# Attention's fill work in a hybrid encoder layer: casts placed behind their loads, the last gate by channels, early sigmoids in stage one, two y tiles kept on chip

## The chip, the cores and the metric

The kernel runs on one core of a Trainium2 chip. Its engines have queues of their own: PE (TensorE) multiplies, ACT (ScalarE) evaluates functions, casts and copies, DVE (VectorE) and POOL (GpSimd) do elementwise work, and SP (SyncE) issues every DMA here, in order. The metric is the device time of one execution in microseconds (us).

## The reference, cut to what matters

One layer with S = D = 1024 and 16 heads of 64. Heads 0 to 7 are softmax heads over a band of keys (branch A), heads 8 to 15 are stick-breaking heads (branch B). Each branch is projected back to 1024 channels and multiplied by a sigmoid gate of its own.

```python
h = x @ w_in[l]
qa, ka, va, qb, kb, vb, ga, gb = jnp.split(h, split_pts, axis=-1)
y_a = chunk_band_attention(heads_a(qa), heads_a(ka), heads_a(va), rel_bias[l]) @ w_proj_a[l]
y_b = stick_breaking_attention(heads_b(qb), heads_b(kb), heads_b(vb)) @ w_proj_b[l]
gate_a = jax.nn.sigmoid(ga + b_gate[l, :D])
gate_b = jax.nn.sigmoid(gb + b_gate[l, D:])
mix = (gate_a * y_a + gate_b * y_b) @ w_out[l]
x = layer_norm(DEEPNORM_ALPHA * x + mix, ln1_g[l], ln1_b[l])
gu = x @ w_ffn_in[l]
g, u = jnp.split(gu, 2, axis=-1)
ffn = (jax.nn.silu(g) * u) @ w_ffn_out[l]
x = layer_norm(DEEPNORM_ALPHA * x + ffn, ln2_g[l], ln2_b[l])
```

A stick-breaking weight is a sigmoid of the score times the running product of one minus the sigmoids between key and query.

## The kernel before, in words

All operands are float32. A product is emulated by three matmuls of the type fp32r: each operand is split into a high part (a cast, on ACT) and a low part (the difference, on DVE or POOL). `split` (L108 to 110) does both. So each weight and each activation tile that PE is to read costs a cast on ACT and a subtraction elsewhere, after its load.

Stage one (0 to some 348 us) projects x to q, k and v of all heads and to ten of the sixteen gate tiles (`project`, `run_pairs`; pairs of column blocks share their seven products as in Strassen's scheme). Results go to DRAM tiles: q_dr, k_dr, v_dr, and g_dr for the gates, as raw sums, by `out_g` (L363 and 364). Its last five pairs are gate pairs, A's tile and B's tile of the same channels c = 0 to 4.

Attention (some 348 to 676 us) goes through the heads in order. One unit computes 128 queries of one head: `scores` (two matmuls, L464 and 465), for a softmax head a bias with a minimum on DVE (L501), exp on ACT (L507) and a division on POOL (L512); for a stick-breaking head two sigmoids on ACT (L539 kp, L540 w), a running product on DVE (L542, L545) and a multiplication on POOL (L547). Then `value_steps` transposes blocks of the weights on PE (`turn`, L570), splits them on ACT and DVE (the pt tiles, L109 and L110), and multiplies by v (`mult`, L583 and 584) into the single PSUM bank pv. At the end of a half the pv bank is copied by ACT (L598; for the last pair L590), half of it changes partitions by DMA (L599), and POOL adds it into the y tile (L602), three steps later, through the list `later`. The finished y tile of a pair of heads, 128 channels by 1024 positions, is stored to y_dr (L604). Pairs 0 to 3 are branch A, 4 to 7 branch B; the last one (y7) stays on chip.

Attention's own PE work leaves PE free, so a generator, `fill_all`, gives PE other matmuls in between; `fill_until` takes from it as many as the constants FILL allow in each step. The fill work is, in this order: the six gate tiles 10 to 15 (`gate`, 48 matmuls each, over eight channels tiles of x), then branch A's projection, eight output tiles c = 0 to 7 of 24 matmuls (L630), each multiplied by its gate gA on DVE (L633). Its inputs come through:

- `load_w`: DMA of a weight tile, the cast (L404) and the subtraction (L405), all emitted at one place. `load_gate` and `load_proj` call it one tile ahead of use.
- `reload_y` (L651 to 657): DMA of a y tile from y_dr, cast on ACT, subtraction on POOL. y0 to y3, branch A's, are reloaded behind gate 15, into the slots that x's split tiles held; y4, y5 and y6 one after each second output tile.
- `reload_gate` (L659 to 662): DMA of a gate tile from g_dr and the sigmoid with its bias on ACT.

After attention, the yB stage (to some 705 us) projects branch B, applies its gates gB through the same `reload_gate`, and adds branch A; then come w_out, LayerNorm, the feed-forward block and the second LayerNorm.

On-chip tiles come from tagged slots (SLOTS) and PSUM banks (BANKS), taken in rotation: who takes a slot waits until its last user is done. Within an engine, instructions run in the order that the scheduler of the framework gives them from the order of the program and its own estimates. So an instruction that waits holds up everything behind it in its engine's queue.

Of the kernel before, what the change touches and what calls it, by code (L numbers as in the profile page):

```python
# [11 lines left out]
F32 = mybir.dt.float32  # L12
F32R = mybir.dt.float32r
AF = mybir.ActivationFunctionType
ALU = mybir.AluOpType
# [32 lines left out]
def hybrid_trunk_kernel(ctx: ExitStack, tc, x, xt, w_in, b_gate, rel_bias, w_proj,  # L48
# [202 lines left out]
    xh = [slot("xt", f"xh{k}", F32R) for k in range(KT)]  # L251
    xl = [slot("xt", f"xl{k}", F32R) for k in range(KT)]
# [72 lines left out]
    def project(i):  # L325
# [37 lines left out]
        def out_g(side):  # L363
            dma(g_dr[2 * pair + int(side) - 1], tl[side])
# [32 lines left out]
    def load_w(srcs, name, raw, hl, lo_eng):  # L397
        r = raw(f"wr_{name}")
        hi = hl(f"wh_{name}", F32R)
        lo = hl(f"wl_{name}", F32R)  # L400
        srcs = srcs if isinstance(srcs, list) else [(slice(0, 1024), srcs)]
        for cs, src in srcs:
            dma(r[:, cs], src)
        nc.scalar.copy(hi, r)  # L404
        lo_eng.tensor_tensor(lo, r, hi.bitcast(F32), ALU.subtract)  # L405
        return hi, lo
# [4 lines left out]
    def load_gate(i, lo_eng):  # L411
        return load_w(w_in[24 + (i % 2) * 8 + i // 2], f"g{i}", of("op"), of("op"), lo_eng)

    def gate(i, w):
        gt = slot("gt", f"gate{i}")
        for hf, cs in enumerate((LO, HI)):
            acc = bank("mm", f"gps{i}_{hf}")
            for k in range(KT):
                ks = slice(k * P, (k + 1) * P)
                for j, (lw, rx) in enumerate(((w[0], xh), (w[0], xl), (w[1], xh))):  # L420
                    mm(acc, lw[:, ks], rx[k][:, cs], start=(k == j == 0),  # L421
                       stop=(k == KT - 1 and j == 2))
                    yield 1.0
            nc.scalar.copy(gt[:, cs], acc)
# [9 lines left out]
    first_w = load_gate(first_gate, nc.vector)  # L434
# [116 lines left out]
    def value_steps(hd, g, wt):  # L551
# [9 lines left out]
        for i, kb in enumerate(kbs):  # L561
# [14 lines left out]
            def mult(i=i, kb=kb, lo_q=lo_q, n=n, pts=pts):  # L576
# [8 lines left out]
                if last:  # L585
# [6 lines left out]
                    else:  # L592
# [8 lines left out]
                        def add():  # L601
                            nc.gpsimd.tensor_tensor(yt[r, gs], yt[r, gs], yv[r, gs], ALU.add)  # L602
                            if h == 1 and g == 1:
                                dma(y_dr[hd["i"]], yt)  # L604
# [6 lines left out]
    def fill_all():  # L611
        w = first_w
        for i in range(first_gate, 16):
            nxt = load_gate(i + 1, nc.gpsimd) if i < 15 else load_proj(0, 0, "op", nc.gpsimd)
            yield from gate(i, w)
            w = nxt
        for i in range(4):
            reload_y(i, nc.gpsimd)
        for cc in range(4):
            nxt = load_proj(0, cc + 1, "op", nc.gpsimd) if cc < 3 else None  # L620
            for j in range(2):
                c = 2 * cc + j
                t = slot("gt", f"gA{c}")
                reload_gate(t, c, 0)
                for hf, cs in enumerate((LO, HI)):
                    acc = bank("mm", f"yAps{c}_{hf}")
# [498 lines left out]
```

## Time and profile before

| what | us |
|---|---|
| median of three runs | 1466.01 |
| lowest, highest | 1466.0, 1467.67 |
| profiled execution | 1465.81 |
| its span | 1464.0 |
| PE busy in the span | 1432.2 |
| ACT busy | 679.4 |
| POOL busy | 278.1 |

The mean granted clock of PE in the profiled execution is 0.995 of full. A line of a timeline reads: start, duration, engine, line of the code, operation, output tile, input tile, shapes, count, and in brackets the idle time of the engine ahead of it with what ended that. A line of the waits reads: who waited for whom, microseconds in total, times, the longest.

### The profile page before, as it was taken

The page shows a single profiled execution, that of the slowest core. Times are in us where ns is not written, and L with a number is a line of the kernel's source. Part 1 is how long each engine was busy: PE and PEld are TensorE (multiplying, and loading weights), DVE is VectorE, ACT ScalarE, POOL GpSimd, SP SyncE. Part 2 cuts the span into 40 slices and gives each one's busy share as a digit, 9 for nine tenths or more (in the row PEclk, how much of TensorE's full clock was granted, in tenths as well). Part 3 has the DMA queues.
Part 4 walks back from the last instruction along what each step waited for, and adds up shares of the span by engine and source line. Part 5 has one row for each costly group of instructions (what it writes and reads, how often), then busy time and mean ns, then how long its engine had stood idle before and what let it go on. Part 6 is the DMA issues. An engine that isn't in the chain of part 4 may idle for free.

```text
span 1464.0 us, 19115 instructions
## 1 busy us (share of the span) xinstructions
PE 1432.2 (98%) x6740; PEld 1184.4 (81%) x6740; DVE 1025.3 (70%) x1637; ACT 679.4 (46%) x1179; POOL 278.1 (19%) x326
## 2 busy tenths in 40 slices
PE   8999999999999998999999999999999999999997
PEld 6788888887888787878888888888888888888886
DVE  8856655434776876887848966777776665978767
ACT  6444444335878878775413534444444433221201
POOL 0000000003555879760004100000000000100016
PEclk9999999999999999999999999999999999999999
DMA  6565545338666476856611123444444457887602
GB/s 216 158 188 173 157 145 177 124 99 249 188 196 206 131 217 184 238 179 247 232 43 72 50 95 130 158 154 148 152 151 145 152 195 247 301 308 235 213 15 101
DMA packets 83455, 247.72 MB, mean 169 GB/s; under 512 B 10512, under 2 KB 10512, under 8 KB 83360
## 3 DMA queue, kind: packets, MB, share of 16 engines
q1 hardware_dynamic: 83360, 246.51, 51.5%
q8 instruction: 53, 0.87, 0.3%
q14 instruction: 42, 0.34, 0.1%
HBM read 162.03 MB, written 80.77 MB: 166 GB/s over the span
## 4 chain that ended last, share of the span: by engine, by line
PE 86%; DVE 5%; DMA 3%; ACT 3%; issue 2%; POOL 1%; SPq 0%; POOLq 0%; DVEq 0%; ACTq 0%
PE sxf L171 16%; PE sxp L171 12%; PE szf L171 8%; PE dx L1058 6%; PE szp L171 6%; PE syf L171 4%; PE gps L421 3%; PE dz L1058 3%; PE syp L171 3%; PE yAps L630 2%; PE ops L117 2%; PE ops L119 2%; PE ops L116 2%; PE fpswh_h L119 1%; PE fpswh_h L116 1%
## 5 line engine op out<-in xcount | busy, mean ns | idle before, releaser
L1014 POOL TENSOR_TENSOR wdyt<-wdyt 128x512 f32<-128x512 f32 x8 | 10.8, 1352 | 513.6 <-DMA wdgt<-in_w_ffn_out_dram 429.1
L547 POOL TENSOR_TENSOR w_b<-w_b,kp_b 128x511 f32<-128x511 f32 (+3 forms) x96 | 96.2, 1010 | 39.0 <-DVE kp_b L542 27.0
L542 DVE TENSOR_TENSOR_SCAN kp_b<-kp_b,ident_ps 128x512 f32<-128x512 f32 (+2 forms) x64 | 56.4, 883 | 24.8 <-ACT kp_b L539 24.3
L482 POOL MEMSET bias<- 64x64 f32 x8 | 1.2, 144 | 329.7 <-ACT bias L481 329.7
L778 POOL TENSOR_TENSOR mv<-mv,neghalf 128x1 f32<-128x1 f32 x16 | 23.8, 1489 | 210.3 <-DVE mv L777 210.3
L184 DVE TENSOR_TENSOR c<-sxp,c 128x512 f32<-128x512 f32 x16 | 11.1, 691 | 74.2 <-issue 41.1
L539 ACT ACTIVATE kp_b<-sc_b 128x512 f32<-128x512 f32 (+3 forms) x96 | 50.0, 521 | 24.9 <-PE sc_b L465 23.2
L110 DVE TENSOR_TENSOR pt_b<-tp_b,pt_b 128x512 fp32r<-128x512 f32 (+1 forms) x96 | 50.4, 543 | 13.8 <-ACT pt_b L109 13.5
L989 DVE TENSOR_TENSOR x<-dx,x 128x512 f32<-128x512 f32 x64 | 43.5, 686 | 17.0 <-PE dx L1058 16.9
L171 PE MATMUL szf<-x1S63h,wcf 128*128 128x512 f32 x168 | 55.1, 389 | 0.0
L109 ACT CAST pt_b<-tp_b 128x512 fp32r<-128x512 f32 (+1 forms) x96 | 48.2, 515 | 7.7 <-PE tp_b L570 6.1
L110 DVE TENSOR_TENSOR sl<-h,sl 128x512 fp32r<-128x512 f32 x56 | 38.4, 685 | 18.8 <-ACT sl L109 18.8
L512 POOL TENSOR_SCALAR w_a<-w_a,st_a 128x640 f32<-128x640 f32 (+2 forms) x64 | 42.6, 670 | 45.1 <-DVE st_a L511 33.5
L109 ACT CAST sl<-h 128x512 fp32r<-128x512 f32 x56 | 34.7, 619 | 34.5 <-PE syf L171 17.1
L110 DVE TENSOR_TENSOR pt_a<-tp_a,pt_a 128x512 fp32r<-128x512 f32 (+1 forms) x96 | 45.8, 486 | 6.8 <-ACT pt_a L109 5.5
L540 ACT ACTIVATE w_b<-sc_b 128x511 f32<-128x511 f32 (+3 forms) x96 | 50.2, 523 | 0.0
L570 PE MATMUL tp_b<-ident,w_b 128*128 128x128 f32 x288 | 48.7, 279 | 1.5 <-DVE pt_b L110 1.1
L116 PE MATMUL ops<-wh_o,mh 128*128 128x512 f32 x128 | 50.2, 392 | 0.0
L119 PE MATMUL ops<-wh_o,ml 128*128 128x512 f32 x128 | 50.0, 391 | 0.0
L117 PE MATMUL ops<-wl_o,mh 128*128 128x512 f32 x128 | 49.9, 390 | 0.0
L109 ACT CAST pt_a<-tp_a 128x512 fp32r<-128x512 f32 (+1 forms) x96 | 39.7, 426 | 19.2 <-PE tp_a L570 17.8
L507 ACT ACTIVATE w_a<-w_a,st_a 128x640 f32<-128x640 f32 (+2 forms) x64 | 44.7, 698 | 6.4 <-DVE st_a L501 5.9
(1883 smaller groups left out, 4811.4 us busy)
## 6 DMA issues: line engine op xcount, KB each, us to landing
s_dr<-sl SPq DMA_DIRECT2D x112, 256.0 KB, 2.1
sd<-s_dr SPq DMA_DIRECT2D x56, 512.0 KB, 4.5
wLf<-in_w_ffn_in_dram SPq DMA_DIRECT2D x22, 512.0 KB, 4.3
wRf<-in_w_ffn_in_dram SPq DMA_DIRECT2D x22, 512.0 KB, 3.6
wLp<-in_w_in_dram SPq DMA_DIRECT2D x17, 512.0 KB, 5.4
wRp<-in_w_in_dram SPq DMA_DIRECT2D x17, 512.0 KB, 4.2
v_dr<-v SPq DMA_DIRECT2D x16, 512.0 KB, 4.6
qs<-q_dr SPq DMA_DIRECT2D x16, 512.0 KB, 5.3
```

What stands on the lines that cost most here:

```text
L109: nc.scalar.copy(dst_h, src)
L110: nc.vector.tensor_tensor(dst_l, src, dst_h.bitcast(F32), ALU.subtract)
L116: mm(acc, lh, rh, start=(i == 0), stop=False)
L117: mm(acc, lh, rl, start=False, stop=False)
L119: mm(acc, ll, rh, start=False, stop=(i == n))
L171: mm(acc, lw[:, ks], rx, start=(first and kt == i == 0), stop=(kt == 3 and i == 2), skip_group_check=not first)
L539: nc.scalar.activation(kp[:, c0:e], sc[:, 0:n], AF.Sigmoid, scale=-1.0)
L540: nc.scalar.activation(be[:, m0:e], sc[:, m0 - c0:n], AF.Sigmoid)
L542: nc.vector.tensor_tensor_scan(kp[:, 0:e], kp[:, 0:e], ident_ps()[:, 0:e], 0.0, ALU.mult, ALU.add)
L547: nc.gpsimd.tensor_tensor(be[:, m0:e], be[:, m0:e], kp[:, m0 - 1:e - 1], ALU.mult)
L570: tr(tp[:, (qb - lo_q) * P:(qb - lo_q + 1) * P], wt[qb - q0][:, (kb - qb) * P:(kb - qb + 1) * P], ident)
L1058: mm(acc, a, b, start=(first and i == n == 0), stop=(i == n - 1 == 1), skip_group_check=not first)
```

## The change

- `load_w` is cut in two: `begin_w` issues the DMA, and the function that it returns emits the cast and the subtraction. For gate weights that function is called half-way through the tile before; for branch A's projection weights at the second output tile of a pair.
- Gate 15 is computed by channels in both of its halves at once, each half in an mm bank. As soon as a channel tile k of x has been used in both, `freed(k)` starts the load of y_k (k below 4), and the split follows two channels later. The split tiles of x are allocated in pairs (xh0, xl0, xh1, ...), so that y_k takes the slots of x's channel k.
- `out_g` applies bias and sigmoid to the ten early gate tiles in stage one, before they are stored; `squash` does it at the reload only for the six tiles from `gate`.
- y5 and y6 are neither stored nor reloaded: they are split from the tile in which POOL's add leaves them, two steps later. y4 is loaded after output tile 0 and split after output tile 1.
- gA tiles are loaded one output tile ahead.

```diff
--- before.py
+++ after.py
@@ -248,8 +248,10 @@
     left(0)
     for k in order_k:
         dma(xraw[k][:, LO], xt[k * P:(k + 1) * P, LO])
-    xh = [slot("xt", f"xh{k}", F32R) for k in range(KT)]
-    xl = [slot("xt", f"xl{k}", F32R) for k in range(KT)]
+    xh, xl = [], []
+    for k in range(KT):
+        xh.append(slot("xt", f"xh{k}", F32R))
+        xl.append(slot("xt", f"xl{k}", F32R))
     for k in order_k:
         split(xh[k][:, LO], xl[k][:, LO], xraw[k][:, LO])
 
@@ -361,6 +363,8 @@
                 dma(v_dr[2 * pr + h].rearrange("p (t c) -> p t c", t=8), vs[h].bitcast(F32))
 
         def out_g(side):
+            col = (int(side) - 1) * 8 + pair
+            nc.scalar.activation(tl[side], tl[side], AF.Sigmoid, bias=bg[:, col:col + 1])
             dma(g_dr[2 * pair + int(side) - 1], tl[side])
 
         out = dict(qk=out_qk, v=out_v, g=out_g)[kind]
@@ -394,34 +398,61 @@
             also(i)
 
 
-    def load_w(srcs, name, raw, hl, lo_eng):
+    def begin_w(srcs, name, raw, hl, lo_eng):
         r = raw(f"wr_{name}")
-        hi = hl(f"wh_{name}", F32R)
-        lo = hl(f"wl_{name}", F32R)
         srcs = srcs if isinstance(srcs, list) else [(slice(0, 1024), srcs)]
         for cs, src in srcs:
             dma(r[:, cs], src)
-        nc.scalar.copy(hi, r)
-        lo_eng.tensor_tensor(lo, r, hi.bitcast(F32), ALU.subtract)
-        return hi, lo
+
+        def end():
+            hi = hl(f"wh_{name}", F32R)
+            lo = hl(f"wl_{name}", F32R)
+            nc.scalar.copy(hi, r)
+            lo_eng.tensor_tensor(lo, r, hi.bitcast(F32), ALU.subtract)
+            return hi, lo
+        return end
+
+    def load_w(*args):
+        return begin_w(*args)()
 
     def of(tag):
         return lambda name, dtype=F32: slot(tag, name, dtype)
 
-    def load_gate(i, lo_eng):
-        return load_w(w_in[24 + (i % 2) * 8 + i // 2], f"g{i}", of("op"), of("op"), lo_eng)
-
-    def gate(i, w):
+    def begin_gate(i, lo_eng):
+        return begin_w(w_in[24 + (i % 2) * 8 + i // 2], f"g{i}", of("op"), of("op"), lo_eng)
+
+    def gate(i, w, half_way, freed=None):
         gt = slot("gt", f"gate{i}")
-        for hf, cs in enumerate((LO, HI)):
-            acc = bank("mm", f"gps{i}_{hf}")
-            for k in range(KT):
-                ks = slice(k * P, (k + 1) * P)
-                for j, (lw, rx) in enumerate(((w[0], xh), (w[0], xl), (w[1], xh))):
-                    mm(acc, lw[:, ks], rx[k][:, cs], start=(k == j == 0),
-                       stop=(k == KT - 1 and j == 2))
-                    yield 1.0
-            nc.scalar.copy(gt[:, cs], acc)
+        acc = [bank("mm", f"gps{i}_{hf}") for hf in range(1 if freed is None else 2)]
+
+        def part(hf, k):
+            ks = slice(k * P, (k + 1) * P)
+            for j, (lw, rx) in enumerate(((w[0], xh), (w[0], xl), (w[1], xh))):
+                mm(acc[hf], lw[:, ks], rx[k][:, (LO, HI)[hf]], start=(k == j == 0),
+                   stop=(k == KT - 1 and j == 2))
+                yield 1.0
+
+        def take(hf):
+            nc.scalar.copy(gt[:, (LO, HI)[hf]], acc[hf])
+
+        if freed is None:
+            for hf in range(2):
+                if hf:
+                    acc.append(bank("mm", f"gps{i}_1"))
+                    half_way()
+                for k in range(KT):
+                    yield from part(hf, k)
+                take(hf)
+        else:
+            half_way()
+            for k in range(6):
+                for hf in range(2):
+                    yield from part(hf, k)
+                freed(k)
+            for hf in range(2):
+                for k in (6, 7):
+                    yield from part(hf, k)
+                take(hf)
         dma(g_dr[i], gt)
 
     left(2)
@@ -431,7 +462,7 @@
     run_pairs([project(i) for i in range(1, len(work))], lambda i: left(i + 1) if i > 1 else None,
               lambda i: right(i + 1), lambda i: small_inputs() if i == 2 else None)
     first_gate = 2 * N_GATE
-    first_w = load_gate(first_gate, nc.vector)
+    first_w = begin_gate(first_gate, nc.vector)()
 
 
 
@@ -601,7 +632,10 @@
                         def add():
                             nc.gpsimd.tensor_tensor(yt[r, gs], yt[r, gs], yv[r, gs], ALU.add)
                             if h == 1 and g == 1:
-                                dma(y_dr[hd["i"]], yt)
+                                if hd["i"] > 4:
+                                    later.append([2, lambda: split_y(hd["i"], yt, nc.gpsimd)])
+                                else:
+                                    dma(y_dr[hd["i"]], yt)
                         later.append([3, add])
 
             steps.append((turn, mult))
@@ -610,20 +644,38 @@
 
     def fill_all():
         w = first_w
-        for i in range(first_gate, 16):
-            nxt = load_gate(i + 1, nc.gpsimd) if i < 15 else load_proj(0, 0, "op", nc.gpsimd)
-            yield from gate(i, w)
-            w = nxt
-        for i in range(4):
-            reload_y(i, nc.gpsimd)
+        got = []
+        for i in range(first_gate, 15):
+            end = begin_gate(i + 1, nc.gpsimd)
+            yield from gate(i, w, lambda: got.append(end()))
+            w = got.pop()
+        end = begin_proj(0, 0, "op", nc.gpsimd)
+        ends = {}
+
+        def freed(k):
+            if k == 0:
+                got.append(end())
+            if k < 4:
+                ends[k] = begin_y(k, nc.gpsimd)
+            if k > 1:
+                ends.pop(k - 2)()
+
+        yield from gate(15, w, lambda: None, freed)
+        w = got.pop()
+        gates = {0: begin_gA(0)}
         for cc in range(4):
-            nxt = load_proj(0, cc + 1, "op", nc.gpsimd) if cc < 3 else None
+            if cc < 3:
+                end = begin_proj(0, cc + 1, "op", nc.gpsimd)
             for j in range(2):
                 c = 2 * cc + j
-                t = slot("gt", f"gA{c}")
-                reload_gate(t, c, 0)
+                t = gates.pop(c)
+                squash(t, c, 0)
+                if c < 7:
+                    gates[c + 1] = begin_gA(c + 1)
                 for hf, cs in enumerate((LO, HI)):
                     acc = bank("mm", f"yAps{c}_{hf}")
+                    if j == 1 and hf == 0 and cc < 3:
+                        got.append(end())
                     for k in range(4):
                         ks = slice(j * HW + k * P, j * HW + (k + 1) * P)
                         for n, (lw, rx) in enumerate(((w[0], yh), (w[0], yl), (w[1], yh))):
@@ -635,31 +687,41 @@
                     dma(m_dr[c], t)
                 else:
                     kept[c] = t
+                if c == 0:
+                    end_y = begin_y(4, nc.gpsimd)
+                elif c == 1:
+                    end_y()
             if cc < 3:
-                reload_y(4 + cc, nc.gpsimd)
-            w = nxt
-
-    def load_proj(br, cc, raw, eng):
-
-        return load_w([(cs, w_proj[2 * cc + j][:, br * HW:(br + 1) * HW])
-                       for j, cs in enumerate((LO, HI))], f"y{br}_{cc}", of(raw), of("op"), eng)
-
+                w = got.pop()
+
+    def begin_proj(br, cc, raw, eng):
+
+        return begin_w([(cs, w_proj[2 * cc + j][:, br * HW:(br + 1) * HW])
+                        for j, cs in enumerate((LO, HI))], f"y{br}_{cc}", of(raw), of("op"), eng)
+
+    def begin_gA(c):
+        t = slot("gt", f"gA{c}")
+        dma(t, g_dr[2 * c])
+        return t
 
     KEEP, kept = 5, {}
     yh, yl = [None] * 8, [None] * 8
 
-    def reload_y(i, eng):
+    def begin_y(i, eng):
         raw = slot("op", f"yraw{i}")
         dma(raw, y_dr[i])
+        return lambda: split_y(i, raw, eng)
+
+    def split_y(i, raw, eng):
         yh[i] = slot("xt", f"yh{i}", F32R)
         yl[i] = slot("xt", f"yl{i}", F32R)
         nc.scalar.copy(yh[i], raw)
         eng.tensor_tensor(yl[i], raw, yh[i].bitcast(F32), ALU.subtract)
 
-    def reload_gate(t, c, br):
-        dma(t, g_dr[2 * c + br])
+    def squash(t, c, br):
         col = br * 8 + c
-        nc.scalar.activation(t, t, AF.Sigmoid, bias=bg[:, col:col + 1])
+        if c >= N_GATE:
+            nc.scalar.activation(t, t, AF.Sigmoid, bias=bg[:, col:col + 1])
 
     fill = fill_all()
     state = dict(t=0.0, done=False)
@@ -746,9 +808,10 @@
     acc_t = [slot(tag, f"acc{tt}") for tt, tag in enumerate(["pt"] * 4 + ["yt"] * 3 + ["bw"])]
     for n, c in enumerate((6, 7, 5, 4, 0, 1, 2, 3)):
         if n % 2 == 0:
-            w = load_proj(1, c // 2, "op", nc.vector)
+            w = begin_proj(1, c // 2, "op", nc.vector)()
         gB = slot("kp", f"gB{c}")
-        reload_gate(gB, c, 1)
+        dma(gB, g_dr[2 * c + 1])
+        squash(gB, c, 1)
         if c in kept:
             mA = kept[c]
         else:
```

## The prediction

> **What bounds the kernel now.** I read the page's busy shares, then TensorE's (PE's) own waits, then stretches of the span, then the timelines of ACT, POOL and PE around the longest gaps.
>
> ```profile
> span 1464.0 us, 19115 instructions
> PE 1432.2 (98%) x6740; PEld 1184.4 (81%) x6740; DVE 1025.3 (70%) x1637; ACT 679.4 (46%) x1179; POOL 278.1 (19%) x326
> ```
> ```profile
> PE pv_b L583 <- ACT yv_b L598: 3.5, 1, 3.5
> PE pv_b L583 <- DVE yt L591: 1.9, 1, 1.9
> PE pv_b L583 <- ACT yt L598: 1.0, 1, 1.0
> PE sc_a L465 <- DMA kl<-k_dr: 1.0, 1, 1.0
> ```
> ```profile
> 100.00:125.00 25.00, 25.00 (x112) 20.71 (x111) 14.06 (x17) 10.11 (x13) 0.00 (x0) 1.00 0.65 196
> ...
> 540.00:560.00 20.00, 20.00 (x115) 17.06 (x113) 14.33 (x21) 16.79 (x39) 15.10 (x21) 1.00 0.62 201
> 560.00:570.00 10.00, 9.59 (x51) 7.57 (x50) 7.86 (x12) 10.00 (x21) 10.00 (x9) 1.00 0.97 234
> ...
> 576.28:583.10 6.82, 5.94 (x19) 5.17 (x20) 4.08 (x7) 5.67 (x12) 6.82 (x7) 0.50 0.19 60
> ...
> 654.78:658.20 3.42, 3.42 (x14) 3.00 (x14) 3.29 (x7) 2.15 (x4) 2.62 (x3) 0.50 0.24 53
> ```
> A stretch's columns are its borders and length, then the busy time of PE, weight load, DVE, ACT and POOL, then the granted clock and the DMA share. PE is the bound, and its work is left as it is. Only waits can be won: three singular ones in late attention and the half clock (0.50) that follows two of them.
>
> **Term 1, y4's cast.** In the order of instructions the cast of y4 goes from behind the pt cast at 570.51 to behind that at 592.47, while its load is issued after the first of branch A's eight output tiles.
>
> ```profile
> 573.26 0.40 PE L630 MATMUL yAps<-yh,wh_y 128*128 128x512 f32 x1
> ...
> 577.16 0.80 PE L583 MATMUL pv_b<-pt_b,v 128*128 128x512 f32 x1 [3.50 <-ACT yv_b L598]
> ```
> ```profile
> 570.51 0.79 ACT L109 CAST pt_b<-tp_b 128x512 fp32r<-128x512 f32 x1
> 575.20 1.04 ACT L656 CAST yh<-yraw 128x1024 fp32r<-128x1024 f32 x1 [3.91 <-DMA yraw<-y_dr]
> ...
> 576.52 0.59 ACT L598 COPY yv_b<-pv_b 128x512 f32<-128x512 f32 x1
> ```
> The page's releaser is the copy at 576.52, but the cause stands two lines above it: ACT stood 3.91 for a load issued just ahead of its cast. From start to start PE lost 573.26 to 577.16 = 3.90, less the 0.22 that a matmul takes in full flow (25.00 for 112 of them from 100 to 125): 3.68. The half clock then stretches 5.94 of work by up to 2.97. Ends 0 (another wait at the same place) and 6.6; I take 6.4 won, since the copy behind the cast has nothing else to wait for.
>
> **Term 2, the wait at 602.**
>
> ```profile
> 602.22 0.40 PE L630 MATMUL yAps<-yh,wh_y 128*128 128x512 f32 x1
> 603.65 0.50 PE L583 MATMUL pv_b<-pt_b,v 128*128 128x512 f32 x1 [1.04 <-ACT yt L598]
> ```
> ```profile
> 599.59 0.62 ACT L109 CAST pt_b<-tp_b 128x512 fp32r<-128x512 f32 x1
> 601.60 1.15 ACT L662 ACTIVATE gA<-gA,bg 128x1024 f32<-128x1024 f32 x1 [1.39 <-DMA gA<-g_dr]
> ```
> PE lost 1.43 - 0.22 = 1.21, and no half clock followed. ACT held the sigmoid for a load of the gate; the gate tiles' loads now go to SP one output tile earlier, and this sigmoid, an early gate's, goes altogether. But in its place the order puts a cast of wh_y whose load is issued about as late. Ends 0 and 1.2; I take 0.7, a little over half.
>
> **Term 3, the wait at 651.** Ahead of it ACT held the y6 cast (648.24) and a cast of wh_y that waited for its load (650.20); both leave.
>
> ```profile
> 651.53 0.40 PE L630 MATMUL yAps<-yh,wl_y 128*128 128x512 f32 x1
> 653.87 0.50 PE L583 MATMUL pv_b<-pt_b,v 128*128 128x512 f32 x1 [1.94 <-DVE yt L591]
> ```
> ```profile
> 645.45 1.15 ACT L662 ACTIVATE gA<-gA,bg 128x1024 f32<-128x1024 f32 x1 [1.36 <-DMA gA<-g_dr]
> ...
> 648.24 1.09 ACT L656 CAST yh<-yraw 128x1024 fp32r<-128x1024 f32 x1
> ...
> 650.20 1.05 ACT L404 CAST wh_y<-wr_y 128x1024 fp32r<-128x1024 f32 x1 [0.49 <-DMA wr_y<-in_w_proj_dram]
> ```
> PE lost 2.34 - 0.22 = 2.12, and half of the 3.42 at half clock is 1.71: 3.8 won; ends 0 and 3.8. The sigmoid at 645.45 belongs to a late gate and stays.
>
> **Term 4, y5 and y6 from the chip.** Two stores and two loads of 512 KB go from SP's queue. Each cast now waits for POOL's add, and ACT's queue stands behind it.
>
> ```profile
> 592.47 0.62 ACT L109 CAST pt_b<-tp_b 128x512 fp32r<-128x512 f32 x1
> 593.32 0.48 ACT L109 CAST pt_b<-tp_b 128x384 fp32r<-128x384 f32 x1 [0.23 <-PE tp_b L570]
> 594.83 0.44 ACT L539 ACTIVATE kp_b<-sc_b 128x320 f32<-128x320 f32 x1 [1.03 <-PE sc_b L465]
> ...
> 635.81 1.14 ACT L109 CAST pt_b<-tp_b 128x512 fp32r<-128x512 f32 x2
> 637.69 0.49 ACT L539 ACTIVATE kp_b<-sc_b 128x384 f32<-128x384 f32 x1 [0.75 <-PE sc_b L465]
> ```
> ```profile
> 592.57 1.28 POOL L602 TENSOR_TENSOR yt<-yt,yv_b 64x512 f32<-64x512 f32 x1 [1.35 <-DMA yt<-yv_b]
> ...
> 638.68 1.29 POOL L602 TENSOR_TENSOR yt<-yt,yv_b 64x512 f32<-64x512 f32 x1
> ```
> ```profile
> L656 ACT CAST yh<-yraw x7: 1045/1095/1232, 551.3 to 648.2; 128x1024 fp32r<-128x1024 f32 x7
> L657 POOL TENSOR_TENSOR yl<-yraw,yh x7: 2371/2397/2400, 554.1 to 649.7; 128x1024 fp32r<-128x1024 f32 x7
> ```
> y6: ACT reaches the cast at 636.95; the add ends at 639.97: 3.0 idle, then 1.05 of cast. Of these 4.1 ACT was idle 0.75 anyway, so kp_b and the score bank behind it are 3.3 late. Behind the cast stand kp_b and w_b of the next block's two score pieces, and behind those the pt casts; the scan, POOL's w_b and PE's transposes wait for them. What PE covers comes from terms 1 and 2: ACT was held up 3.91 + 1.04 there and PE lost 3.68; it was held up 1.39 + 1.15 and PE lost 1.21; 1.3 was covered each time. So 2.0 lost. Ends: 0.3, if the lead of the scores covers 3, and 3.3 + 1.7 of half clock = 5.0. I take 2.0. y5: ACT at 593.09, add to 593.85: 0.8, two casts (y5, y4) 2.1, less 1.3 that ACT was idle anyway (1.03 + 0.23), less 1.3 covered: 0.3 lost; ends 0 and 1.6. POOL then does yl5 and yl4 (4.8) ahead of its next w_b; if that is late, the turns (transposes) and so PE wait: that is why the upper end stays at 1.6.
>
> The clock's rule in the Trainium skill ("TensorE: Matmul & The Clock Gate", Part 1) asks for some 3.4 us of idle window before the clock halves. The trace disagrees in part: 3.68 was followed by 0.50, but 2.12 too, and 1.21 was not. By the page y6's 2.0 brings no half clock, the first rival below loses its 1.7 and the sum stands; by the row at 651 it brings 1.7 more loss.
>
> **Term 5, y0 to y3 and gate 15 by channels.** Four ACT casts (4.4) and four POOL subtractions (9.6) move some 11 us earlier, into 540 to 551. PE was full in 540 to 560, and lost 0.41 in 560 to 570, where ACT and POOL were full. Gate 15 goes through its channels once, in both column halves together, so that x's first channels come free early; its 48 matmuls are the same, and the bank that it holds longer is free again before branch A starts. ACT had 3.2 free of 20 in that window, POOL 4.9, so nearly all fits. Ends +0.4 and -1.2 (what one operation held up ahead of a pt cast cost at 602); I take +0.2, by the full PE. If the cover is gone, the four casts are 4.4 late on ACT, 3.1 after the 1.3.
>
> **Term 6, the start of attention.** The last two sigmoids stand ahead of their stores, which stand ahead of kl, v and a gate's weights on SP, and exp needs its table again. The casts of a gate's weights move to the middle of the gate before.
>
> ```profile
> 344.04 1.05 ACT L404 CAST wh_g<-wr_g 128x1024 fp32r<-128x1024 f32 x1 [3.59 <-DMA wr_g<-in_w_in_dram]
> ...
> 348.51 1.05 ACT L404 CAST wh_g<-wr_g 128x1024 fp32r<-128x1024 f32 x1
> 349.67 0.83 ACT L507 ACTIVATE w_a<-w_a,st_a 128x640 f32<-128x640 f32 x1
> ...
> 469.18 1.28 ACT L539 ACT_TABLE_LOAD   x1
> 470.47 0.60 ACT L539 ACTIVATE kp_b<-sc_b 128x512 f32<-128x512 f32 x1
> ```
> ```profile
> L662 ACT ACTIVATE gA<-gA,bg x8: 1151/1154/1463, 565.1 to 645.4; 128x1024 f32<-128x1024 f32 x8
> ```
> One sigmoid and the table are 1.15 + 1.28 = 2.4 ahead of the first exp; the cast at 348.51 goes behind, -1.05: 1.4 late. Ends: +1.0, if kl's wait vanishes because more gate matmuls stand ahead of it, and -3.0, the 2.4 and half of 1.15 that kl's store waits. I take -0.7, half of 1.4, as about 1.3 was covered elsewhere but here PE starts without a lead. The later gates' casts move beside a PE that was full (540 to 560): 0.
>
> The Trainium skill ("ScalarE: Activation LUTs", What ACT_TABLE_LOAD costs) adds a drain of 1.38 to each 1.28. The trace has the next activation 0.01 behind the load at 469.18; by the page this term would be 1.4 worse, and the time 1459.1.
>
> **Term 7, the sigmoids of stage one.** Eight more of 1.15 and one table load of 1.28, beside PE at 25.00 of 25.00 and ACT at 10.11: 0 lost, ends 0 and -1. Without that cover they would cost 10.5. The ten that go were 1.15 each; the one of them that stood for its load ahead of a PE gap is term 2's, and the yB stage behind them is PE's: 0.
>
> **Sum**: 6.4 + 0.7 + 3.8 - 2.0 - 0.3 + 0.2 - 0.7 + 0 = 8.1. The profiled execution took 1465.81 (0.2 below the median of 1466.01): 1457.7.
>
> **The rivals.**
> *The wait changes hands.* y6's cast makes a gap with half clock: 5.0 for 2.0, so 1460.7. For it: 636.95 against 639.97, and the half clock after 2.12. Against it: kp_b was early there.
> *Slower: ACT behind POOL.* Both casts wait for an add that POOL, with 2.4 each for the yl ahead, does late; ACT late makes scans late and POOL later. If each costs what 573 did (6.4), the loss is 12.8 for 2.3: 1468.2. It decides from 10.4 for both together. For it: POOL at 10.00 of 10.00 in 560 to 570. Against: at 592.57 the add waited for its DMA, not POOL.
> *The backlog only moves.* ACT and POOL keep their work but for the sigmoids; with the load's wait gone PE meets the next one (the pv bank, a late w_b) a little further on. If a gap like that at 651 is left at both places, with its half clock (2.12 + 1.71), term 1 falls from 6.4 to 2.6 and term 3 to 0: 8.1 - 3.8 - 3.8 = 0.5, so 1465.3. For it: ACT and POOL full from 560 to 570, and POOL 6.82 of 6.82 at the half clock. Against it: the 14 us of term 5's casts and subtractions leave just that stretch.
> *All gains, no losses*: 6.6 + 1.2 + 3.8 + 0.4 + 1.0, less y6's 0.3 = 12.7: 1453.1.
>
> **How the numbers follow.** Forecast 0.52 (own range 1454 to 1460: up by 1.7 of y6, 1.7 of the start and 0.5 of term 2; down by 2.3 of the start), wait changes hands 0.20, slower 0.12, backlog moves 0.12, all gains 0.04. What a measurement tells from no change is 0.2%, 2.9 us. Faster: 0.52 + 0.20 + 0.04 = 0.76; same 0.12; slower 0.12. The range 1453.5 to 1465.5 leaves out the slower case and most of the last, some 0.15.
>
> **What would show it.** Right: no 3.9 wait for yraw on ACT, no clock of 0.50 near 576 and 655, PE's waits for yv_b and for DVE yt under 1 each, a new row of ACT yh waiting for POOL yt of some 3.0, the first exp 1 to 2 later. Wrong: a PE gap over 2 near 638 or 594 with half clock behind it, a kl wait over 2, or gaps in stage one where PE was full.

## The result, and the profile after

The changed kernel takes 1456.48 us (median of 5 runs, 1455.94 to 1459.09) against 1466.01 (5 runs, 1464.64 to 1467.67): the ratio is 0.994, with a 95% interval of 0.9926 to 0.9953. The forecast was 1457.7. Its profiled execution took 1455.94, with a span of 1454.0: 10.0 us less than before, where the medians differ by 9.5.

The page's shares of the changed kernel:

```profile
span 1454.0 us, 19114 instructions
...
PE 1426.7 (98%) x6740; PEld 1180.2 (81%) x6740; DVE 1024.0 (70%) x1637; ACT 682.6 (47%) x1181; POOL 279.2 (19%) x326
```

The longest of PE's waits after its first matmuls, and what stood in their place:

```profile
PE tp_b L601 <- DVE pt_b L110: 3.4, 5, 1.0
PE sc_a L495 <- DVE st_a L532: 1.8, 6, 0.3
...
PE sc_b L495 <- ACT w_b L571: 0.4, 1, 0.4
```

The four waits that the prediction quoted are gone: pv_b for ACT's yv_b, for ACT's yt and for DVE's yt, and kl. No stretch at half clock is left ahead of the last 6 us of the span. Stretches of the changed kernel (length, then PE, weight load, DVE, ACT, POOL, granted clock, DMA share):

```profile
560.00:570.00 10.00, 10.00 (x57) 8.53 (x56) 7.83 (x12) 7.51 (x19) 10.00 (x14) 1.00 0.95 307
...
575.00:600.00 25.00, 24.07 (x138) 20.52 (x137) 20.95 (x31) 20.90 (x46) 23.77 (x26) 1.00 0.78 221
...
625.00:650.00 25.00, 22.89 (x127) 18.50 (x125) 20.24 (x29) 18.25 (x41) 15.90 (x19) 1.00 0.45 161
650.00:675.00 25.00, 24.79 (x124) 19.56 (x123) 15.85 (x26) 12.19 (x20) 0.00 (x0) 1.00 0.57 206
```

Only 625 to 650 has a loss worth the name. ACT's timeline there and at 585, the new waits for POOL's add:

```profile
585.41 1.05 ACT L718 CAST yh<-yt 128x1024 fp32r<-128x1024 f32 x1 [0.39 <-POOL yt L633]
...
631.66 1.05 ACT L718 CAST yh<-yt 128x1024 fp32r<-128x1024 f32 x1 [3.04 <-POOL yt L633]
```

Where the time went can be read from instructions that both traces have in the same order. The scores' matmuls of attention are such; the table compares when the n-th of them starts, in us. A last column that falls is time won, one that rises is time lost.

| instruction | before | after | after less before |
|---|---|---|---|
| first score matmul | 347.82 | 347.73 | -0.09 |
| 113th score matmul | 414.27 | 413.40 | -0.87 |
| 289th | 555.83 | 555.13 | -0.69 |
| 313th | 585.83 | 577.76 | -8.07 |
| 321st | 594.28 | 586.22 | -8.06 |
| 329th | 601.31 | 594.23 | -7.07 |
| 353rd | 625.34 | 616.58 | -8.76 |
| 377th | 648.24 | 642.51 | -5.73 |
| first matmul of the yB stage | 675.42 | 665.57 | -9.85 |

So 0.8 came at the start of attention, 7.4 between 556 and 586, 1.7 between 601 and 625 (after 1.0 had been lost at y5's cast), 3.0 was lost at y6's cast, and 4.1 came at 651.

### The profile page after: what moved, and what is told of

The parts are those of the page before. It is cut to its first block, busy times and chain, and to the rows that moved or that the text cites. A ratio compares the mean times of both kernels' runs of the same rounds, so it can differ in the third digit from the quotient of the medians.

```text
span 1454.0 us, 19114 instructions
## 1 busy us (share of the span) xinstructions
PE 1426.7 (98%) x6740; PEld 1180.2 (81%) x6740; DVE 1024.0 (70%) x1637; ACT 682.6 (47%) x1181; POOL 279.2 (19%) x326
## 4 chain that ended last, share of the span: by engine, by line
PE 87%; DVE 7%; ACT 2%; issue 2%; DMA 1%; POOL 1%; SPq 0%; POOLq 0%; DVEq 0%; ACTq 0%
PE sxf L171 15%; PE sxp L171 12%; PE szf L171 8%; PE szp L171 6%; PE dx L1121 6%; PE syf L171 4%; PE gps L431 4%; PE dz L1121 3%; PE syp L171 3%; PE yAps L682 2%; PE tp_b L601 2%; PE ops L117 2%; PE ops L119 2%; PE ops L116 2%; PE dy L1121 1%
```

## The experiments

All are compared by their medians and by the 95% interval of their ratio to the kernel before, which was measured again beside each group of them (medians 1466.2 for runs 1, 2, 6 and 8, 1465.7 for 3, 4, 9 and 10, 1465.42 for 5, 7 and 11). Between two of these runs a difference of about 1 us is within their spread. What PE lost in a gap is counted as in the prediction, from start to start less the time of the matmul in full flow. The theory at first was that of the prediction: the 573 gap comes from where y4's cast stands.

**1. y4's cast later, alone.** The edit is in `split` and in `reload_y` of the kernel before: `pts` keeps the casts that `split` makes, and `issue_after` queues what follows behind such a cast on ACT, without any other wait.

```diff
-        nc.scalar.copy(dst_h, src)
+        pts.append(nc.scalar.copy(dst_h, src).ins)
...
-        nc.scalar.copy(yh[i], raw)
+        with tc.issue_after(pts[-1]) if i == 4 else ExitStack():
+            nc.scalar.copy(yh[i], raw)
```

> The kernel before with one edit: ACT's cast of y4 is queued behind the pt cast that was emitted last, some 15 us later; its load stays. Theory (the cast that stood in ACT's queue just behind its own load made the 573 gap): the wait of 3.9 for yraw goes, PE's 3.68 and the half clock behind it go, 6.4 in all: 1459.6; the gaps at 602 (1.2) and 651 (2.1 with half clock) stay. Rival (ACT's and POOL's backlog only moves): another gap of about 2.1 with half clock appears within 20 us, gain 2.6 or less: 1463.4 or more.

1465.75 (ratio 0.9987 to 1.0005): nothing was won. ACT's timeline of this run:

```profile
575.13 1.04 ACT L406 CAST wh_y<-wr_y 128x1024 fp32r<-128x1024 f32 x1 [3.61 <-DMA wr_y<-in_w_proj_dram]
...
593.60 1.09 ACT L659 CAST yh<-yraw 128x1024 fp32r<-128x1024 f32 x1
```

The y4 cast went to 593.60 without a wait, and the next weight's cast stepped into its place and waited 3.61 for a load that landed at 575 as well. PE lost 2.56 and 0.75 there and the half clock came, as the rival had it. In this trace 1.7 was won between the 289th and the 313th score matmul, and 1.2 was lost again between 601 and 612, in gaps where PE waited for ACT. The theory fell: the cast's place alone was not the cause. The loads were late, and whichever cast came next waited.

Why they were late stands in the waits of SP's queue in the kernel before (from 535 to 600), its timeline and POOL's:

```profile
SPq L403 <- POOL yl L657: 5.5, 1, 5.5
...
SPq L403 <- POOL wl_y L405: 3.3, 1, 3.3
SPq L653 <- POOL yl L657: 2.3, 1, 2.3
```
```profile
556.56 0.81 SPq L403 DMA_DIRECT2D wr_y<-in_w_proj_dram  x2
...
568.19 0.33 SPq L653 DMA_DIRECT2D yraw<-y_dr  x1
571.86 0.81 SPq L403 DMA_DIRECT2D wr_y<-in_w_proj_dram  x2
```
```profile
554.13 2.40 POOL L657 TENSOR_TENSOR yl<-yraw,yh 128x1024 fp32r<-128x1024 f32 x1
...
565.77 2.40 POOL L657 TENSOR_TENSOR yl<-yraw,yh 128x1024 fp32r<-128x1024 f32 x1
...
569.42 2.41 POOL L405 TENSOR_TENSOR wl_y<-wr_y,wh_y 128x1024 fp32r<-128x1024 f32 x1
```

A raw tile's slot is free when its subtraction is done. y0's ends at 556.53 and SP issues a weight's load at 556.56; y3's ends at 568.17 and y4's load goes out at 568.19; the weight's ends at 571.83 and the next load goes out at 571.86. In the changed kernel the same queues read:

```profile
544.35 1.35 SPq L405 DMA_DIRECT2D wr_y<-in_w_proj_dram  x2
548.77 0.33 SPq L712 DMA_DIRECT2D yraw<-y_dr  x1
...
566.46 1.69 SPq L405 DMA_DIRECT2D wr_y<-in_w_proj_dram  x2
```
```profile
541.91 2.41 POOL L719 TENSOR_TENSOR yl<-yraw,yh 128x1024 fp32r<-128x1024 f32 x1
...
546.34 2.40 POOL L719 TENSOR_TENSOR yl<-yraw,yh 128x1024 fp32r<-128x1024 f32 x1
```

There y4's load goes out 19.4 us earlier, at the end of y1's subtraction, and the next weight's at 566.46 in place of 571.86. The new theory: gate 15 by channels lets y0 to y3 be split early, that releases the slots, and the loads are no longer late.

**2. The changed kernel with gate 15 whole.** In `fill_all`, `freed` leaves with it.

```diff
-        yield from gate(15, w, lambda: None, freed)
+        yield from gate(15, w, lambda: got.append(end()))
+        for k in range(4):
+            begin_y(k, nc.gpsimd)()
```

> The changed kernel with gate 15 computed half by half again, as the other gates, and y0 to y3 loaded and split behind it. Theory (term 5, worth +0.2): the four casts return to 551 to 560 before PE's first yAps, the 0.4 at 565 and the POOL backlog to 575 return, but y4's cast stays far behind, so no long gap: 0 to 1.5 slower than the changed kernel, 1456.5 to 1458. Rival (the POOL backlog from 554 to 583 is part of the 573 gap, and the early casts are what took it away): a gap of 2 or more near 575 to 580 returns, with half clock, 1460 or more.

1464.6 (ratio 0.9982 to 0.9999): 8.1 slower than the changed kernel, as the rival had it, though no single gap reached its 2. ACT's timeline:

```profile
577.42 1.05 ACT L410 CAST wh_y<-wr_y 128x1024 fp32r<-128x1024 f32 x1 [5.24 <-DMA wr_y<-in_w_proj_dram]
...
594.16 1.05 ACT L711 CAST yh<-yt 128x1024 fp32r<-128x1024 f32 x1 [3.19 <-POOL yt L633]
```

PE lost 1.85, 1.54 and 1.16 between 574 and 580, and the clock halved; then 1.76 and 1.60 between 594 and 600 from y5's cast, and it halved again. Against the changed kernel 6.3 was lost between the 289th and the 313th score matmul and 4.8 more up to the 329th. The loads were late once more, but not for a raw slot alone: y4's load went out at 564.53, and the weight's at 572.10 stood in SP's queue behind a load of gA at 571.68, whose wait the trace puts down to a gate's store.

**3. Gate 15 by channels alone**, put into the kernel before, with y0 to y3 loaded and split during it; the core of the edit:

```diff
+        for k in range(6):
+            for hf in range(2):
+                yield from part(hf, k)
+            if k < 4:
+                ends[k] = begin(k)
+            if k > 1:
+                end(k - 2, ends.pop(k - 2))
...
-        for i in range(4):
-            reload_y(i, nc.gpsimd)
```

> The kernel before with gate 15 by channels and y0 to y3 loaded and split during it, and nothing else of the change. New theory (early splits release the raw slots some 12 us sooner, which is most of the gain): the 573 gap and its half clock go, the gaps at 602 (0 to 1.2) and at 651 (2.1 with half clock) stay: 1458 to 1460.5. Rival (the parts work only together): 1463 or more.

1461.88 (0.9969 to 0.9987). Between the 289th and the 313th score matmul it gains 7.4 on the kernel before, as much as the whole change gains there. It does not show that the slots alone did it. The subtraction of y3 ended at 558.10, but y4's load went out only at 566.26, 1.9 earlier than in the kernel before, because a gate's store (564.55) stood ahead of it in SP's queue. And the cast of y4, though the program asks for it at the same point, came to stand three microseconds further back in ACT's queue, behind the copy of pv:

```profile
570.53 0.62 ACT L109 CAST pt_b<-tp_b 128x512 fp32r<-128x512 f32 x1
...
572.84 0.57 ACT L636 COPY yv_b<-pv_b 128x512 f32<-128x512 f32 x1
...
574.52 1.08 ACT L695 CAST yh<-yraw 128x1024 fp32r<-128x1024 f32 x1
```

The earlier load and the later place came together here. At 596 the run gives 2.6 back:

```profile
596.83 1.15 ACT L701 ACTIVATE gA<-gA,bg 128x1024 f32<-128x1024 f32 x1 [2.80 <-DMA gA<-g_dr]
```

PE came there earlier, the gate's load did not, the wait that was 1.39 became 2.80, PE's gap 1.21 became 2.64, and that brought a half clock. So the expectation's 573 part held and its 602 part was too low.

**4. The subtractions of y0 to y3 on DVE**, in the kernel before.

```diff
-            reload_y(i, nc.gpsimd)
+            reload_y(i, nc.vector)
```

> The kernel before with one edit: the subtractions of y0 to y3 run on DVE (1.23 each) instead of POOL (2.40 each); the orders of ACT and SP stay as they were, y4's cast stands in its old place. New theory (SP issues the loads of y4 and of the projection weights only when POOL's subtraction has released a raw slot, so they land at 575, and whichever cast is next on ACT waits): the slots come free 4 to 6 us sooner, y4's load is issued near 563 in place of 568.2, ACT's wait of 3.9 and PE's gap at 573 with its half clock go: 1458.5 to 1461. Old theory of the prediction (the cast's place in the queue): no change, 1465 to 1466.5. Rival (DVE is too full there and delays the scans): slower than 1466.5.

1462.85 (0.9974 to 0.9991). The 573 gap and its half clock went, but not as expected: y4's load was issued at 568.21, as before, behind a gate's store in SP's queue, and PE fell 2.4 further behind the kernel before in five gaps of 0.60 to 0.75 between 555 and 569, so that it reached the place later. The four subtractions took 1.55, 1.74, 1.20 and 2.00 on DVE, not the 1.23 that was expected. From the 289th to the 313th score matmul the gain is 4.8. The run shows what small gaps are worth beside one long one; on the slots it decides nothing.

**5. Two subtractions on DVE**, those that release the slots of the two late loads.

```diff
-            reload_y(i, nc.gpsimd)
+            reload_y(i, nc.vector if i == 3 else nc.gpsimd)
-            nxt = load_proj(0, cc + 1, "op", nc.gpsimd) if cc < 3 else None
+            nxt = load_proj(0, cc + 1, "op", nc.gpsimd if cc else nc.vector) if cc < 3 else None
```

> The kernel before with two subtractions on DVE in place of POOL, those that release the slots of y4's and of the third projection weight's loads (y3's, and the second projection weight's); the orders of ACT and SP stay. Theory (late release, late load, ACT waits): SP issues y4's load near 566 and the weight's near 567 in place of 568.2 and 571.9, ACT's wait for yraw falls from 3.9 to 2 or less, PE's gap at 573 stays under 2 and no half clock follows, while the two subtractions (1.25 each) cost DVE's scans 0 to 1: 1459.5 to 1461.5. Rival (in the run with four on DVE the gap went only because PE was some 2.4 late already): the gap stays above 2.1 with half clock, 1464 or more.

1466.3 (0.999 to 1.0013): a miss. The gap at 573 came some eight us earlier, by PE's timeline, because y3's subtraction took 5.66 on DVE in place of 1.25 and a pt split stood behind it; DVE's and POOL's timelines follow:

```profile
569.73 0.55 PE L570 MATMUL tp_b<-ident,w_b 128*128 128x128 f32 x3 [4.13 <-DVE pt_b L110]
```
```profile
563.41 5.66 DVE L657 TENSOR_TENSOR yl<-yraw,yh 128x1024 fp32r<-128x1024 f32 x1
568.99 0.68 DVE L110 TENSOR_TENSOR pt_b<-tp_b,pt_b 128x512 fp32r<-128x512 f32 x1
569.59 1.21 DVE L405 TENSOR_TENSOR wl_y<-wr_y,wh_y 128x1024 fp32r<-128x1024 f32 x1
```
```profile
563.15 2.39 POOL L657 TENSOR_TENSOR yl<-yraw,yh 128x1024 fp32r<-128x1024 f32 x1
565.50 2.48 POOL L547 TENSOR_TENSOR w_b<-w_b,kp_b 128x511 f32<-128x511 f32 x2
```

The half clock followed. POOL worked without a break from 563.15 to 567.98, and DVE's subtraction ended 1.08 after that. The long ones of run 4 (1.55, 1.74 and 2.00) and two of the kernel before (1.94 at 651.28, 1.36 at 658.27) likewise ended 1.04 to 1.09 after the end of an operation on POOL, while beside an idle POOL this subtraction takes 1.22. Where POOL's operation began after it, as at 569.59, it kept its 1.21. So in these traces work that is moved from POOL to DVE can still wait for POOL; what ties them was not tried by itself. y4's load went out at 571.73, later than before, so the run decides nothing on the slots. This trace had also lost 2.3 at the start, in a gap at kl with a half clock.

**6. Raw gates**, the sigmoids back at the reload, all else as changed.

```diff
-            col = (int(side) - 1) * 8 + pair
-            nc.scalar.activation(tl[side], tl[side], AF.Sigmoid, bias=bg[:, col:col + 1])
...
-        if c >= N_GATE:
-            nc.scalar.activation(t, t, AF.Sigmoid, bias=bg[:, col:col + 1])
+        nc.scalar.activation(t, t, AF.Sigmoid, bias=bg[:, col:col + 1])
```

> The changed kernel with the ten early gates stored raw and their sigmoids back at the reload, all else as changed. Theory (they are free in stage one, and late attention's ACT has little room): the start gets its first exp 1.4 earlier, which PE hardly feels (0 to 0.5 faster), five sigmoids of 1.15 return to ACT between 565 and 645 and cost PE 0 to 1.3 each where a pt cast waits behind them, 1 to 3 in all: 1457 to 1459. Rival A (prediction's term 6: table and sigmoids cost 0.7 or more at the start and nothing is won later): 1455 to 1456. Rival B (the sigmoids are what made the late gaps): a gap with half clock returns near 592 to 600, 1460 or more.

1458.87 (0.9941 to 0.9964), 2.4 slower than the changed kernel by the medians, as the theory had it; the ranges of the two overlap (1457.24 to 1460.57 here). From the first score matmul to the 289th it gains 0.4, after it loses 2.2 in gaps of up to 1.56, none with half clock. The gap at 602 does not come back, though the sigmoid does, and the sigmoid there (598.90) waits for no load: gA tiles are loaded one output tile ahead.

**7. The sigmoids alone**, put into the kernel before by the two edits that 6 takes back.

> The kernel before with the ten early sigmoids in stage one and nothing else of the change. Theory (by the run with raw gates, the sigmoids are worth 2 in late attention where the casts are early; here the late load still stands at 573): 573 stays with half clock, the sigmoid that waits at 601 for its load goes and with it 0 to 1.2, small gaps at 590 and 630 shrink; 1463.5 to 1465.5. Rival A (they cost 0.7 or more at the start and win nothing): 1466.5 or more. Rival B (ACT's room is the root of the 573 gap): the gap goes, 1460 or less.

1463.16 (0.9965 to 0.9985), a little better than expected. The gap at 602 went; the one at 573 shrank to 2.16, still with half clock, because y4's cast waited 2.61 in place of 3.91, by ACT's timeline:

```profile
573.28 1.04 ACT L658 CAST yh<-yraw 128x1024 fp32r<-128x1024 f32 x1 [2.61 <-DMA yraw<-y_dr]
```

Rival A falls: the start lost nothing.

**8. The casts of y5 and y6 later**, in `split_y` of the changed kernel; `pts` is as in 1. y4's cast, which stands behind y5's, goes back with it.

```diff
-        nc.scalar.copy(yh[i], raw)
+        with tc.issue_after(pts[-1]) if i > 4 else ExitStack():
+            nc.scalar.copy(yh[i], raw)
```

> The changed kernel with the casts of y5 and y6 queued on ACT behind the pt cast two transposes later, so that POOL's add is done when ACT gets there. Theory (ACT's wait of 3.0 for the add at 631 costs PE 2.6 to 3.0 in three small gaps, the one at 585 about 1.0 at 590): ACT's wait for POOL yt goes, the gaps at 629 to 635 shrink to under 1 in sum, 2 to 3.5 us faster than the changed kernel: 1453 to 1454.5. Rival (the cost is POOL's 2.4 us subtractions that stand ahead of its w_b, wherever the cast stands): within 1 us of the changed kernel, 1455.5 to 1457.5.

1456.17 (0.9923 to 0.9947): as the rival's number had it, but not for its reason. Against the changed kernel 0.8 was won at y5 and 1.9 at y6, and 4.3 was lost from 601 on in this trace:

```profile
602.66 1.04 ACT L412 CAST wh_y<-wr_y 128x1024 fp32r<-128x1024 f32 x1 [3.40 <-DMA wr_y<-in_w_proj_dram]
```

y4's subtraction had moved back with the casts, its raw slot came free later, and SP's second half of that weight's load went out at 597.46 in place of 595.64: PE lost 2.62 and the half clock came.

**9. y6's cast alone later** (as 8, with `i == 6`).

> The changed kernel with y6's cast alone queued two pt casts later; nothing else moves on ACT, SP or PE. Theory: ACT's wait of 3.0 for POOL's add goes, PE's three gaps there shrink by 2.0: 1453.8 to 1455.2. Rival (POOL's subtraction of y6 costs the same wherever it stands): 1456 to 1457.

1455.22 (0.9916 to 0.9939): 1.3 less than the changed kernel. From the 353rd to the 377th score matmul it loses 1.2 on the kernel before where the changed kernel loses 3.0. The median stands at the edge of what was expected.

**10. All three casts placed**: as 8 with `i > 3`, and y4's split asked for half a tile sooner.

```diff
+                    if c == 1 and hf == 1:
+                        end_y()
...
-                elif c == 1:
-                    end_y()
```

> The changed kernel with all three loose casts placed: y4's in ACT's idle second behind the second transposes of pair 5's last head and its subtraction ahead of yl5, y5's and y6's two pt casts later than now. Theory: 2.0 for y6 and 0.8 to 1.0 for y5, with the weight loads no later than in the changed kernel: 1453 to 1454. Rival (a load of projection weights becomes late, as when y4's subtraction was pushed back): a gap with half clock near 600, 1456 or more.

1454.05 (1453.82 to 1455.1 in 5 runs; ratio 0.9909 to 0.9935), the best of all: 2.4 less than the changed kernel's median and 12 less than the kernel before. Its casts of y4, y5 and y6 wait for nothing:

```profile
582.75 1.05 ACT L721 CAST yh<-yraw 128x1024 fp32r<-128x1024 f32 x1
586.76 1.06 ACT L721 CAST yh<-yt 128x1024 fp32r<-128x1024 f32 x1
...
633.56 1.05 ACT L721 CAST yh<-yt 128x1024 fp32r<-128x1024 f32 x1
```

The intervals of its ratio and the changed kernel's overlap a little; the ranges of their runs do not.

**11. y5 and y6 by DRAM**, in the kernel of 10.

```diff
-                                if hd["i"] > 4:
-                                    later.append([2, lambda: split_y(hd["i"], yt, nc.gpsimd)])
-                                else:
-                                    dma(y_dr[hd["i"]], yt)
+                                dma(y_dr[hd["i"]], yt)
...
-                    if c == 1 and hf == 1:
+                    if c in (1, 3, 6) and hf == 1:
...
-                if c == 0:
-                    end_y = begin_y(4, nc.gpsimd)
+                if c in (0, 2, 5):
+                    end_y = begin_y({0: 4, 2: 5, 5: 6}[c], nc.gpsimd)
```

> The best version so far (all three casts placed) with y5 and y6 stored to DRAM and loaded again, their casts queued well behind the loads. Theory (keeping them on chip saves DMA traffic that nobody waits for, but also keeps two loads out of SP's queue and two raw slots free): weight loads behind y5's come later, a cast of a weight may wait 0 to 3 for its load: 0 to 4 slower than the version it is made from, 1454 to 1458. Rival A (on chip is worth most of the change's gain): 1460 or more. Rival B (on chip costs, by the casts that wait for POOL): faster than 1453.

1455.59 (0.9913 to 0.9938), by the medians 1.5 more than 10 and 0.9 less than the changed kernel. Neither difference is clear: by the ratios to the kernel before it is 0.4 more than 10 (0.9925 against 0.9922), and the ranges of the runs overlap both ways. So the four transfers of 512 KB are worth little; PE's gaps at 641 (1.62) and 650 (1.13) are new with them.

## Why the prediction was right

The time was 1.2 under the forecast, and most terms came near the size that was given, but the largest one had the wrong cause. That this did not show in the sum is luck: the edit that term 1 credited and the one that won the time, in term 5, are both part of the change.

- **Terms 1 and 5.** Together 6.6 was forecast and 7.4 measured (from -0.69 to -8.07). The division was wrong: term 1 gave 6.4 to the place of y4's cast "since the copy behind the cast has nothing else to wait for", and term 5 gave 0.2 to gate 15 by channels. Run 1 moved the cast alone and won nothing in the median; run 3 took the channels alone and won 7.4 at this place; run 2 took them away and lost 6.3 there, with 4.8 more at y5's cast in its trace. The step that failed is the reading of the bracket at 575.20: it names the load that ACT waited for, and the argument stopped there, without asking SP's queue why the load was late and what else was late with it. What run 1 did to the gap is the rival "the backlog only moves". The prediction named its sign, ACT and POOL full from 560 to 570, and set against it that term 5's casts and subtractions leave that stretch. That argument held, but it was the larger part of the gain and stood in term 5 with 0.2.
- **Term 2.** 0.7 forecast, 1.7 measured between 601 and 625 (from -7.07 to -8.76): 1.2 of it is the gap at 602, the term's upper end, and the rest are small waits up to 611 that it did not have. Both of its edits would do: raw gates with loads one tile ahead had no such gap (run 6), and early sigmoids alone had none (run 7). Its price also depended on term 1: with PE earlier and the load not, the gap grew to 2.64 with half clock (run 3).
- **Term 3.** 3.8 forecast, 4.1 measured (from -5.73 to -9.85), 0.7 of it a smaller gap at 649 that the term did not name. Right in kind and near in size.
- **Term 4.** y6: 2.0 lost by forecast, 3.0 measured (from -8.76 to -5.73); ACT's wait was 3.04, as worked out from the two rows at 636.95 and 639.97. The cover of 1.3 was too much there: PE's gaps of 0.87, 0.58 and 1.17 are 2.6 of the 3.0. y5: 0.3 forecast, 1.0 measured. Run 10 shows that 1.8 of y6's 3.0 and all of y5's 1.0 were the casts' place in the queue, not the keeping on chip.
- **Term 6.** -0.7 forecast, +0.8 measured (from -0.09 to -0.87). The term's upper end came, not the value that was taken: PE's gap at kl is gone in all seven traces with the early sigmoids, which have two gaps of 0.5 or less near 356 and 361, and it stands in all six without them, with 0.50, 1.00, 1.14, 1.55 and 1.67, and in run 5 with 3.01. With that spread the 0.8 of one pair of traces is no price of the sigmoids; run 6, without them, came to the 113th score matmul 0.4 sooner after the first than the changed kernel. The first exp came 1.34 later (351.01 against 349.67), as worked out, and PE filled that time with gate matmuls.
- **Term 7.** 0 forecast, 0.09 gained at the first score matmul, which is nothing: over all the traces it starts between 347.21 and 348.51. Right: PE was 25.00 of 25.00 beside the sigmoids.
- **The rivals.** The slower one asked for 10.4 at y5 and y6 and they cost 4.0. In run 2, where the add came later (ACT waited 3.19 for it in place of 0.39), y5's cast brought two gaps and a half clock, so it was nearer than its 0.12 looks.
- **The table's drain.** The trace has the exp at 351.01, right behind its table load of 349.72 with 1.28. The 1.38 that the Trainium skill adds ("ScalarE: Activation LUTs", What ACT_TABLE_LOAD costs) is not seen here either, and the 1459.1 of that sentence was too high.

Left open: that gate 15 by channels wins the time at 573 is shown by putting it in (run 3) and by taking it out (run 2). How it does so is argued. That raw slots held the loads back is read from SP's waits in the kernel before; in run 3 the load was 1.9 earlier and the cast also stood further back, in run 2 the weight's load waited for something else, and runs 4 and 5 changed DVE's load and do not isolate the slots. No run has the loads earlier with the order on ACT kept. What the later casts of the gates' and projection weights do was not tried alone.

## What to carry to other kernels

A bracket that says "waited for a DMA" is the middle of a chain: look in the issuing queue when the load went out and what it waited for there. In run 1 the cast that the bracket named was moved away, and the next instruction that needed a late load waited in its place. Fixing one wait with others right behind it shows little; it pays to find what they share. And a cast that needs another engine's last result should be queued behind work that is ready, which is a matter of the queue's order, not only of where the program asks for it (runs 8 to 10; in run 3 the order moved though the program asked at the same place).

## What was not expected of the hardware

The half clock comes in whole windows. In the kernel before the two stretches begin at 576.28 and 654.78, 78.50 apart, which is 23 windows of 3.413; in run 2 they begin at 580.73 and 601.21, 20.48 apart, which is 6. How busy PE was in the window ahead goes with it. Stretches of run 1, of the kernel with raw gates, of run 2 and of run 5, cut at such windows (columns as above):

```profile
574.39:577.80 3.41, 0.93 (x5) 0.34 (x3) 1.09 (x1) 2.67 (x6) 3.41 (x5) 1.00 0.42 144
577.80:581.22 3.42, 2.92 (x10) 2.63 (x11) 3.35 (x7) 2.62 (x7) 3.34 (x4) 0.50 0.14 59
649.48:652.90 3.42, 1.47 (x8) 0.91 (x7) 3.42 (x3) 2.45 (x7) 1.04 (x1) 1.00 0.59 217
652.90:656.31 3.41, 3.41 (x14) 3.09 (x13) 3.34 (x7) 1.64 (x4) 2.34 (x3) 0.50 0.18 34
```
```profile
635.42:638.83 3.41, 1.99 (x10) 1.04 (x9) 3.13 (x4) 3.41 (x10) 3.41 (x5) 1.00 0.88 315
638.83:642.25 3.42, 3.42 (x20) 2.88 (x19) 3.14 (x6) 2.36 (x6) 3.06 (x5) 1.00 0.00 0
```
```profile
573.90:577.31 3.41, 1.72 (x13) 1.35 (x12) 0.00 (x0) 0.00 (x0) 3.41 (x5) 1.00 0.70 262
577.31:580.73 3.42, 1.10 (x7) 0.52 (x5) 1.84 (x4) 3.31 (x9) 3.32 (x3) 1.00 0.00 0
597.79:601.21 3.42, 1.78 (x11) 1.34 (x11) 3.21 (x7) 2.47 (x8) 3.42 (x2) 1.00 0.23 90
601.21:604.62 3.41, 3.41 (x13) 2.82 (x13) 1.80 (x3) 1.98 (x4) 3.41 (x8) 0.50 0.76 229
```
```profile
652.57:655.98 3.41, 1.54 (x8) 0.99 (x6) 3.11 (x3) 3.14 (x8) 1.77 (x1) 1.00 0.88 255
655.98:659.39 3.41, 3.32 (x20) 2.82 (x21) 3.41 (x7) 1.78 (x4) 1.62 (x2) 1.00 0.04 18
```

With 0.93, 1.10 and 1.47 busy of 3.41 the next window was at half, with 1.99 it was not; in run 2 the one of 1.78 was followed by half and the one of 1.72 by full clock, and in run 5 the one of 1.54 by full clock. So the edge lies between 1.47 and 1.99 and is not sharper in these rows. At half clock it is another one: in the kernel before, the window at 576.28 was busy for 2.53, and the next was at half again. The Trainium skill ("TensorE: Matmul & The Clock Gate", Part 1) has the same free-running window of 3413 ns, and the grid agrees; but the window need not be idle: the clock halved each time in all these traces where 1.47 or less of 3.41 was busy. So a gap of 2.1 within one window cost up to 1.7 more, the gaps of 1.54 and 1.16 in one window of run 2 did the same, and run 4's five gaps of 0.60 to 0.75, spread over 14 us, left the clock full.
